# Linear attention's own-tile products as four products of 64 stationary columns a tile

## The chip, the cores and the metric

The kernel runs on one core of one Trainium2 chip. The metric is the device time of one execution, in microseconds (us). Five engines matter here: PE (TensorE: matrix products into PSUM, with its weight loads shown apart as PEld), DVE (VectorE), ACT (ScalarE), POOL (GpSimd) and SP, which issues the DMAs. A product on PE takes a stationary operand, loaded into the array (its columns become the rows, that is the partitions, of the result), and a moving operand, whose columns are streamed past it. A product whose stationary operand has 64 columns occupies one half of the array's columns and writes 64 of the 128 partitions of PSUM.

## What is computed

The reference is a layer of a diffusion backbone: 512 latent tokens and 256 context tokens of width 1024 go through one input projection, then through two branches (latent attention, and bidirectional gated linear attention with 4 heads of key and value width 128), a merge, and a gated MLP with a convolution. The change lies in the linear attention. One direction of it, for one head, cut to what matters:

```python
b_cum = jnp.cumsum(to_chunks(g), axis=3)          # log decay inside a chunk
decay, u = chunk_state_terms(kc, vc, b_cum)
s_final, s_in = scan_states(decay, u, s0)
qe = qc * jnp.exp(b_cum)
mask = jnp.tril(jnp.ones((GLA_CHUNK, GLA_CHUNK), jnp.float32))
a = jnp.einsum('bhncd,bhnsd->bhncs', qe, kc * jnp.exp(-b_cum)) * mask
o = jnp.einsum('bhncs,bhnsv->bhncv', a, vc) + jnp.einsum('bhncd,bhndv->bhncv', qe, s_in)
```

Both directions are added: a token attends forward to the tokens before it and backward to those after it, and to itself twice. The part that a chunk takes from itself (`a`) is what is called the own-tile products below; the rest comes through the state `s_in`.

## The kernel before

The kernel computes the layer in stages, each bound together by the planner of the language: `TC_KW = {"schedule_with_timeline_sim": True}` (L1562) has the order of the instructions on each engine planned from modelled costs, except where an engine's name stands in `pinned` (program order is kept) or in `behind` (instructions are put behind a named one). In the linear attention's stage nothing is pinned any more; PE's instructions only stand behind one early product (L1265). Large projections use operands split in a high and a low part; the products of the linear attention itself are plain fp32, and each of those shows as two MATMULs (two passes) with a weight load each.

The loop over the four heads (L1270 on) calls, for each head: `states`, which makes the states of both directions at the borders of the four 128-token tiles (PE products into PSUM tile `p`, ACT copies, then six DVE steps into tile `S`); `output`, which the change touches; `decay` of the next head (two scans on DVE and exponentials on ACT); projections and gates (`merge_mla`, `proj_kq`, `gate`); `gate_out`; `apply` and `to_tokens` of the next head.

`output` works on tiles of 128 tokens, as two halves c0 and c1 of 64. `K[:, 0]` and `K[:, 1]` are the keys of the forward and the backward direction (in the trace `T`), `Qp[:, 0]` and `Qp[:, 1]` the queries (in the trace `s`), all with the 128 key channels on the partitions. For each tile it makes a 128x128 block, keys on the rows and queries on the columns. The block of c0 keys and c1 queries is forward alone, that of c1 keys and c0 queries backward alone; in the two diagonal blocks both directions are needed, so there the backward product goes into `xp` and the forward one into `yp`. DVE then multiplies `xp` by `twice_diag` into `Am` (in the trace `w`), and two masked copies (COPY_PREDICATED) put the forward values of `yp` in place where the key comes before the query. Last, for each tile, the output `op` is the sum of two products of the queries `Qi` with the states (`pb<-S,s`) and one of `Am` with the values (`pb<-s,w`).

In lines L1198 to L1204 each tile has five products: one with all 128 stationary columns (`K[:, 1, cs]`) and 64 moving columns, and four with 64 stationary and 64 moving columns. In the trace these are `p<-s,T 128*128 128x64` and `p<-s,T 128*64 128x64`; the number before the star is the contraction, the number behind it the stationary columns, and the last number the moving columns.

Of the kernel before, what the change touches and what calls it, by code (L numbers as in the profile page):

```python
# [13 lines left out]
ALU = mybir.AluOpType  # L14
# [56 lines left out]
def block_kernel(ctx: ExitStack, tc: tile.TileContext, p, out):  # L71
# [3 lines left out]
    class Engine:  # L75
# [5 lines left out]
        def __getattr__(self, op):  # L81
            fn = getattr(self.eng, op)

            def call(*args, **kw):
                if self.name in behind:
                    with tc.issue_after(behind[self.name].ins):
# [6 lines left out]
    V, A, G, PE, SY = (Engine("V", nc.vector), Engine("A", nc.scalar), Engine("G", nc.gpsimd),  # L93
                       Engine("PE", nc.tensor), Engine("SY", nc.sync))
    cnt = [0]

    def tl(pool, shape, dt, tag, bufs=None):
        cnt[0] += 1
        kw = {} if bufs is None else {"bufs": bufs}
        return pool.tile(shape, dt, name=f"{tag}_{cnt[0]}", tag=tag, **kw)  # L100
# [8 lines left out]
    def pb():  # L109
        return tl(psp, [128, 512], F32, "pb", 4)  # L110

    def p2():
        return tl(psp, [128, 1024], F32, "p2", 2)
# [7 lines left out]
    def sm(n, tag, bufs=2):  # L121
        return tl(small, [128, n], F32, tag, bufs)
# [10 lines left out]
    def tt(eng, out_, a, b, op):  # L133
        return eng.tensor_tensor(out=out_, in0=a, in1=b, op=op)
# [14 lines left out]
    def mm(o, a, b, first=True, last=True):  # L149
        PE.matmul(o, lhsT=a, rhs=b, start=first, stop=last)  # L150
# [4 lines left out]
    def grp(ap, a):  # L155
        return ap.rearrange("p (a b) -> p a b", a=a)

    def rep(ap, a):

        return ap.rearrange("p (a b) -> p a b", a=1).broadcast_to([ap.shape[0], a, ap.shape[1]])  # L160

    def each(ap, n):

        return ap.rearrange("p (a b) -> p a b", b=1).broadcast_to([ap.shape[0], ap.shape[1], n])
# [19 lines left out]
    def rstd_exp(ss, n, inv_n, v=None):  # L184

        r, t = sm(n, f"rr{n}"), sm(n, f"rt{n}")
        if v is None:
            v = sm(n, f"rv{n}")
            V.tensor_scalar(out=v, in0=ss, scalar1=-0.5 * inv_n, scalar2=-0.5 * EPS, op0=ALU.mult, op1=ALU.add)
        A.activation(r, v, AF.Ln, scale=-2.0)  # L190
        A.activation(r, r, AF.Exp, scale=-0.5)
        if n == 1:
            V.tensor_scalar(out=t, in0=r, scalar1=r, scalar2=v, op0=ALU.mult, op1=ALU.mult)
            V.tensor_scalar(out=r, in0=t, scalar1=1.5, scalar2=r, op0=ALU.add, op1=ALU.mult)
        else:
            tt(V, t, r, r, ALU.mult)
            tt(V, t, t, v, ALU.mult)
            V.scalar_tensor_tensor(out=r, in0=t, scalar=1.5, in1=r, op0=ALU.add, op1=ALU.mult)
        return r
# [26 lines left out]
    twice_diag = cst[:, 130:258]  # L226
# [108 lines left out]
    with tc.tile_pool(name="e1", bufs=1) as e1:  # L335
# [309 lines left out]
        for j in range(1, 8):  # L645
            n = j + 1
# [419 lines left out]
    with tc.tile_pool(name="egl", bufs=1) as eg:  # L1066
# [9 lines left out]
        def w2():  # L1076
            return tl(eg, [128, 512], F32, "w2", 2)
# [73 lines left out]
        def vh(h, t):  # L1151
            return glav[t // 2][:, t % 2, h * 128:(h + 1) * 128]
# [35 lines left out]
        def output(h, dec, Q, St):  # L1188

            K = dec[1]
            Qp, Qi = Q
            xy = p2()
            xp, yp = xy[:, 0:512], xy[:, 512:768]
            for t in range(4):
                c0, c1 = slice(t * 128, t * 128 + 64), slice(t * 128 + 64, t * 128 + 128)
                cs = slice(t * 128, t * 128 + 128)  # L1198
                mm(xp[:, c0], K[:, 1, cs], Qp[:, 1, c0])
                mm(xp[0:64, c1], K[:, 0, c0], Qp[:, 0, c1])  # L1200
                mm(xp[64:128, c1], K[:, 1, c1], Qp[:, 1, c1])
                ys = slice(t * 64, t * 64 + 64)
                mm(yp[0:64, ys], K[:, 0, c0], Qp[:, 0, c0])
                mm(yp[64:128, ys], K[:, 0, c1], Qp[:, 0, c1])  # L1204
            Am = w2()
            tt(V, grp(Am, 4), grp(xp, 4), rep(twice_diag, 4), ALU.mult)
            for hf in range(2):
                rw = slice(64 * hf, 64 * hf + 64)
                V.copy_predicated(grp(Am, 4)[rw, :, rw], below.bitcast(I32).rearrange("p (a b) -> p a b", a=1)[rw]
                                  .broadcast_to([64, 4, 64]), grp(yp[rw, :], 4))  # L1210
            op = pb()
            for t in range(4):
                cs = slice(t * 128, (t + 1) * 128)
                mm(op[:, cs], Qi[:, 0, cs], St[:, 0, t, :], True, False)
                mm(op[:, cs], Qi[:, 1, cs], St[:, 1, t, :], False, False)
                mm(op[:, cs], Am[:, cs], vh(h, t), False, True)
            on = w2()
            A.activation(on, op, AF.Square)
            so = sm(4, "so")
            V.tensor_reduce(out=so, in_=grp(on, 4), op=ALU.add, axis=AX.X)  # L1220
            ro = rstd_exp(so, 4, 1.0 / 128)
            tt(V, grp(on, 4), grp(op, 4), each(ro, 128), ALU.mult)
            return on
# [46 lines left out]
        for h in range(GH):  # L1270
            St = states(h, dec)
            on = output(h, dec, Q, St)
            if h + 1 < GH:
                dec = decay(h + 1)
                merge_mla(2 * h)
                mod_end()
                kq = proj_kq(h + 1)
            else:
                merge_mla(2 * h)
                mod_end()  # L1280
                mod_begin(S4f)
                merge_mla(2 * h + 1)
            gate_out(h, on, gr)
            if h + 1 < GH:
                Q = apply(kq, dec)
                gr = gate(h + 1)
                to_tokens(dec)
                mod_begin(S4f)
                merge_mla(2 * h + 1)
# [138 lines left out]
    with tc.tile_pool(name="eff", bufs=1) as ef:  # L1428
# [82 lines left out]
        for t in range(4):  # L1511
# [8 lines left out]
            for i, (a, b) in enumerate(parts):  # L1520
# [11 lines left out]
                else:  # L1532

                    cs = slice(t * 128, (t + 1) * 128)
# [49 lines left out]
```

## Time and profile before

| | |
|---|---|
| median of three runs | 907.14 us (907.0 to 908.59) |
| the profiled execution's own time | 906.93 us |
| its span, from the first to the last instruction | 905.1 us |
| PE busy | 889.3 us, 98% of the span |
| DVE, ACT, POOL busy | 577.2, 395.8, 370.5 us |
| granted clock of PE | 0.998 of full speed |

The times of rows are those of the one profiled execution, in microseconds from the start of its span. The own time is the span and 1.8 us around it. A busy share is an average; what a change in one stage is worth is read from the waits and the order of time in that stage.

### The profile page before, as it was taken

What the parts mean: (1) busy time and instruction counts of PE and PEld (TensorE: products, weight loads), DVE (VectorE), ACT (ScalarE), POOL (GpSimd) and SP (SyncE); (2) the same over time, 40 slices, a digit from 0 to 9 for tenths busy, and PEclk for the clock granted to TensorE, in tenths of its full rate; (3) what the DMA queues carried; (4) which work ended last, traced back from release to release, by engine and by line L of the source; (5) the groups of instructions that cost most, each with busy time, mean ns of one, the idle gap of its engine ahead of it and who ended that gap; (6) DMA issues with size and microseconds to landing.
All of it is one profiled execution on the core that took longest, in us unless ns stands there. A gap on an engine that the chain in (4) does not pass through costs nothing.

```text
span 905.1 us, 12711 instructions
## 1 busy us (share of the span) xinstructions
PE 889.3 (98%) x4902; PEld 753.4 (83%) x4902; DVE 577.2 (64%) x970; ACT 395.8 (44%) x655; POOL 370.5 (41%) x223
## 2 busy tenths in 40 slices
PE   8999999999999999999999999999999999999996
PEld 6888899888888888888887899888888888888885
DVE  4477788775878686846774684987777776300006
ACT  4355676764353545434544333443333333322105
POOL 2512364640625252524653424343444444466403
PEclk9999999999999999999999999999999999999999
DMA  9950001224314242325972413434343432244002
GB/s 325 307 145 1 1 7 31 71 84 150 105 35 128 59 128 59 117 59 184 316 246 80 117 47 108 126 93 140 93 140 94 140 116 94 79 155 150 34 1 93
DMA packets 131436, 100.89 MB, mean 111 GB/s; under 512 B 6826, under 2 KB 121874, under 8 KB 131376
## 3 DMA queue, kind: packets, MB, share of 16 engines
q1 hardware_dynamic: 130256, 97.56, 34.9%
q0 software_dynamic: 864, 2.22, 0.7%
q8 instruction: 38, 0.62, 0.3%
q10 hardware_dynamic: 256, 0.30, 0.1%
q14 instruction: 22, 0.18, 0.1%
HBM read 97.78 MB, written 2.10 MB: 110 GB/s over the span
## 4 chain that ended last, share of the span: by engine, by line
PE 92%; DVE 3%; ACT 2%; issue 1%; POOL 1%; DMA 1%; SPq 0%; ACTq 0%; DVEq 0%; POOLq 0%
PE pb L88 49%; PE p L88 23%; PE pb L87 14%; PE p L87 6%; DMA raw<-in_w_ada_dram 1%; DVE s L88 1%; ACT P L88 0%; DVE kT L88 0%; DVE mx L88 0%; ACT s L88 0%; DVE P L88 0%; POOL P L88 0%; POOL s L88 0%; POOL wlo L88 0%; ACT kT L88 0%
## 5 line engine op out<-in xcount | busy, mean ns | idle before, releaser
L88 POOL TENSOR_TENSOR wlo<-raw,whi 128x1024 fp32r<-128x1024 f32 (+1 forms) x106 | 241.3, 2283 | 350.8 <-ACT whi L88 339.1
L88 PE MATMUL pb<-s,whi 128*128 128x512 f32 (+1 forms) x906 | 272.1, 383 | 0.0
L88 PEld LDWEIGHTS pb<-s,whi 128*128 128x128 f32 x906 | 167.3, 188 | 32.2
L88 ACT CAST whi<-raw 128x1024 fp32r<-128x1024 f32 (+1 forms) x106 | 103.2, 975 | 177.9 <-issue 78.2
L88 PE MATMUL pb<-s,wlo 128*128 128x512 f32 (+1 forms) x453 | 172.8, 381 | 0.0
L88 DVE SCALAR_TENSOR_TENSOR ac<-pb,cwT,ac 128x441 f32<-128x441 f32 (+2 forms) x160 | 110.9, 693 | 19.3 <-ACT ac L88 15.5
L87 PE MATMUL pb<-s,whi 128*128 128x512 f32 x320 | 101.8, 396 | 0.0
L88 PEld LDWEIGHTS pb<-s,wlo 128*128 128x128 f32 x453 | 85.2, 188 | 16.6
L88 PE MATMUL p<-s,s 128*128 128x512 f32 (+1 forms) x392 | 82.8, 367 | 0.6 <-DVE s L88 0.5
L88 PEld LDWEIGHTS p<-s,s 128*128 128x128 f32 x392 | 65.8, 189 | 14.0 <-issue 2.1
L87 PEld LDWEIGHTS pb<-s,whi 128*128 128x128 f32 x320 | 58.9, 188 | 12.4 <-issue 0.7
L88 PE MATMUL p<-whi,s 128*128 128x512 f32 x208 | 69.0, 393 | 0.1
L88 DVE TENSOR_TENSOR p<-p,gt 128x512 f32<-128x512 f32 x4 | 2.8, 699 | 98.5 <-PE p L88 98.4
L87 PE MATMUL pb<-s,wlo 128*128 128x512 f32 x160 | 62.8, 392 | 0.0
L88 PE MATMUL pb<-whi,s 128*128 128x512 f32 x176 | 57.6, 390 | 0.0
L88 PEld LDWEIGHTS p<-whi,s 128*128 128x128 f32 x208 | 39.0, 188 | 8.5 <-ACT s L88 0.4
L88 DVE TENSOR_TENSOR pl<-pb,ph 128x512 fp32r<-128x512 f32 x48 | 33.0, 687 | 14.8 <-ACT ph L88 14.5
L88 PE MATMUL p<-kT,s 128*128 128x512 f32 (+1 forms) x192 | 41.1, 350 | 0.9 <-ACT P L88 0.9
L88 PE MATMUL pb<-s,s 128*32 128x128 f32 (+2 forms) x322 | 41.1, 315 | 0.3 <-DMA s<-in_w_ada_dram 0.3
L88 PE MATMUL p<-wlo,s 128*128 128x512 f32 x104 | 40.5, 389 | 0.0
L88 ACT ACTIVATE ac<-ac 128x512 f32<-128x512 f32 x22 | 13.9, 632 | 60.5 <-DVE ac L88 60.5
L88 PEld LDWEIGHTS pb<-whi,s 128*128 128x128 f32 x176 | 33.1, 188 | 6.9
(248 smaller groups left out, 1564.3 us busy)
## 6 DMA issues: line engine op xcount, KB each, us to landing
raw<-in_w_up_dram SPq DMA_DIRECT2D x44, 512.0 KB, 3.7
raw<-in_w_in_dram SPq DMA_DIRECT2D x28, 512.0 KB, 3.7
raw<-in_w_down_dram SPq DMA_DIRECT2D x22, 512.0 KB, 3.6
s<-in_w_ada_dram SPq DMA_DIRECT2D x20, 512.0 KB, 5.8
raw<-in_w_ada_dram SPq DMA_DIRECT2D x18, 512.0 KB, 5.1
xn<-in_w_ada_dram SPq DMA_DIRECT2D x10, 512.0 KB, 4.8
kT<-in_w_in_dram SPq DMA_DIRECT2D x8, 320.0 KB, 6.8
s<-in_x_dram SPq DMA_DIRECT2D x4, 512.0 KB, 4.9
```

The lines of the kernel that those rows point to most:

```text
L87: return fn(*args, **kw)
L88: ins = fn(*args, **kw)
```

## The change

The five products of a tile become four, all with 64 stationary columns, written alternately to the upper and the lower half of the partitions. The product with 128 stationary columns is cut in its two halves; its upper half (c1 keys, c0 queries) is joined with the backward product of the c1 diagonal block to one product of 128 moving columns, and the forward products of c0 keys with c0 and with c1 queries are joined likewise. The results of a tile stand in 256 columns of PSUM instead of 192, so the two kinds of result are no longer in two tiles `xp` and `yp`, and the DVE multiplication and the two masked copies read them with other strides. Their number, their shapes and the values are the same.

```diff
             K = dec[1]
             Qp, Qi = Q
-            xy = p2()
-            xp, yp = xy[:, 0:512], xy[:, 512:768]
+
+            xy = grp(p2(), 4)
+            lo_, hi_ = slice(0, 64), slice(64, 128)
             for t in range(4):
+                xt = xy[:, t, :]
                 c0, c1 = slice(t * 128, t * 128 + 64), slice(t * 128 + 64, t * 128 + 128)
                 cs = slice(t * 128, t * 128 + 128)
-                mm(xp[:, c0], K[:, 1, cs], Qp[:, 1, c0])
-                mm(xp[0:64, c1], K[:, 0, c0], Qp[:, 0, c1])
-                mm(xp[64:128, c1], K[:, 1, c1], Qp[:, 1, c1])
-                ys = slice(t * 64, t * 64 + 64)
-                mm(yp[0:64, ys], K[:, 0, c0], Qp[:, 0, c0])
-                mm(yp[64:128, ys], K[:, 0, c1], Qp[:, 0, c1])
+                mm(grp(xt[hi_, :], 2)[:, :, lo_], K[:, 1, c1], Qp[:, 1, cs])
+                mm(xt[lo_, 64:192], K[:, 0, c0], Qp[:, 0, cs])
+                mm(xt[hi_, 64:128], K[:, 0, c1], Qp[:, 0, c1])
+                mm(xt[lo_, 0:64], K[:, 1, c0], Qp[:, 1, c0])
             Am = w2()
-            tt(V, grp(Am, 4), grp(xp, 4), rep(twice_diag, 4), ALU.mult)
+            tt(V, Am.rearrange("p (t b n) -> p t b n", t=4, b=2),
+               xy.rearrange("p t (b u n) -> p t b u n", b=2, u=2)[:, :, :, 0, :],
+               twice_diag.rearrange("p (t b n) -> p t b n", t=1, b=2).broadcast_to([128, 4, 2, 64]), ALU.mult)
             for hf in range(2):
                 rw = slice(64 * hf, 64 * hf + 64)
                 V.copy_predicated(grp(Am, 4)[rw, :, rw], below.bitcast(I32).rearrange("p (a b) -> p a b", a=1)[rw]
-                                  .broadcast_to([64, 4, 64]), grp(yp[rw, :], 4))
+                                  .broadcast_to([64, 4, 64]), xy[rw, :, 64:128])
```

## Rows read from the trace of the kernel before

**Rows 1.** The page: busy time of each engine, and PE's granted clock in slices.

```profile
PE 889.3 (98%) x4902; PEld 753.4 (83%) x4902; DVE 577.2 (64%) x970; ACT 395.8 (44%) x655; POOL 370.5 (41%) x223
PEclk9999999999999999999999999999999999999999
```

**Rows 2.** Waits of PE, whole kernel: who waited for whom, us, times, longest.

```profile
PE p L88 <- DVE s L88: 2.2, 3, 1.8
...
PE p L87 <- ACT T L88: 1.0, 1, 1.0
```

**Rows 3.** The chain that ended last, in order of time: start, us, what.

```profile
300.03 5.02 PE p L87 x60
305.06 4.83 PE pb L87 x22
```

**Rows 4.** Busy time of each engine from one head's products to the next's.

```profile
255.29:302.10 46.81, 46.81 (x276) 39.62 (x275) 34.74 (x53) 23.20 (x38) 17.12 (x8) 1.00 0.28 80
302.10:348.92 46.82, 46.82 (x276) 39.63 (x275) 34.72 (x53) 23.20 (x38) 18.46 (x9) 1.00 0.32 90
348.92:395.76 46.84, 46.84 (x276) 39.63 (x275) 34.80 (x54) 22.78 (x38) 18.65 (x9) 1.00 0.29 86
```

**Rows 5.** PE groups by shape, whole kernel: count, busy us, mean ns, idle before.

```profile
L87 PE MATMUL p<-s,T 128*64 128x64 f32 x128 | 7.2, 234 | 0.0
...
L87 PE MATMUL p<-s,T 128*128 128x64 f32 x32 | 6.6, 286 | 0.0
```

**Rows 6.** PE timeline, head 0, narrow looks: start, first start to last end, count.

```profile
255.18 0.33 PE L87 MATMUL p<-s,T 128*128 128x128 f32 x2
255.35 0.28 PE L87 MATMUL p<-s,T 128*128 128x64 f32 x1
255.56 0.28 PE L87 MATMUL p<-s,T 128*64 128x64 f32 x2
255.66 0.34 PE L87 MATMUL p<-s,T 128*64 128x64 f32 x6
255.94 0.32 PE L87 MATMUL p<-s,T 128*128 128x64 f32 x1
256.10 0.48 PE L87 MATMUL p<-s,T 128*128 128x64 f32 x3
256.30 0.28 PE L87 MATMUL p<-s,T 128*64 128x64 f32 x2
257.80 0.45 PE L87 MATMUL p<-s,T 128*64 128x64 f32 x8
258.18 0.49 PE L87 MATMUL pb<-S,s 128*128 128x128 f32 x2
```

**Rows 7.** PE timeline just before them: passes of 128 moving columns, 128 stationary.

```profile
253.62 0.72 PE L87 MATMUL p<-s,T 128*128 128x128 f32 x5
```

**Rows 8.** PE timeline in an early stage: 32 stationary and 128 moving columns.

```profile
15.51 0.32 PE L88 MATMUL pb<-s,s 128*32 128x128 f32 x4
15.51 0.65 PE L88 MATMUL pb<-s,s 128*32 128x128 f32 x16
```

**Rows 9.** DVE timeline around head 0's products: start, us, idle before.

```profile
255.96 1.64 DVE L88 SCALAR_TENSOR_TENSOR S<-S,ml,p 128x128 f32<-128x128 f32 x6 [1.07 <-ACT S L88]
258.30 0.69 DVE L88 TENSOR_TENSOR w<-p,cst 128x512 f32<-128x512 f32 x1 [0.70 <-PE p L87]
259.02 0.90 DVE L88 COPY_PREDICATED w<-cst,p 64x256 f32<-64x256 int32 x2
```

**Rows 10.** PE timeline, head 0: the first product that reads `Am`.

```profile
264.44 0.38 PE L87 MATMUL pb<-s,w 128*128 128x128 f32 x2
```

## The prediction

> **What bounds the kernel now.** I read the page first, then PE's waits, the chain in order of time, and at last the stretch itself. The page has PE busy for 889.3 of 905.1 us at full granted clock, with no slice below it; no other engine comes near [rows 1]. That alone would not say that PE sets the time in the linear attention, so the second view is that of PE's waits: over the whole kernel the longest sum is 2.2 us, and the one wait of line 87, where this stage's PE instructions stand, is 1.0 us, once [rows 2]. The chain that ended last runs through PE in this stage with no other engine between, the 60 MATMULs that hold the states' and the own-tile products among its pieces [rows 3]. And from the start of one head's products to the next's PE is busy for 46.81 of 46.81, 46.82 of 46.82 and 46.84 of 46.84 us, while DVE has 34.7 to 34.8, ACT about 23 and POOL 17 to 19 [rows 4]. So a microsecond taken from PE here is a microsecond of the span, as long as nobody else becomes late.
>
> How much PE time the products have is in the groups by shape: 128 passes of 64 stationary columns, 7.2 us, and 32 of 128 columns, 6.6 us [rows 5]; 13.8 us in four heads. Although they are a quarter as many, the whole ones take nearly as much. The last view shows why.
>
> **What a tile costs now.** The narrow looks give starts [rows 6]. The pass of the whole product at 255.35 is followed by a pair of half ones at 255.56: 0.21 us, where a pass of 64 columns has 0.06 in a run of such passes (below). So 0.15 us goes into the change from 128 to 64 stationary columns. The two passes of the pair start within 0.01 us of each other: they are on the two halves of the array and run at once. The next passes start at 255.66, 0.10 later; six of them end 0.34 later, and one lasts 0.22 (its group's mean is 0.234 [rows 5]), so three pairs start within 0.12 us: 0.06 a pair. The first pair costs 0.10 because its weight load has nothing to hide behind; after that the loads are hidden. From the last pair, at 255.66 + 0.12 = 255.78, to the next whole product at 255.94 is 0.16, of which about 0.10 is the change back. Its two passes lie 0.16 apart (255.94 and 256.10), again with a first load in the open, and the next pair is at 256.30. A tile lasts from 255.56 to 256.30, or by three tiles (255.56 to 257.80) 0.747 us: 0.10 + 0.06 + 0.06 + 0.16 for the halves and 0.16 + 0.21 for the whole product. All of it, from the last pass of the states at 255.18 to the first product with the states at 258.18, is 3.00 us.
>
> **What a tile costs after.** Each half of the array gets one product of 128 and one of 64 moving columns, that is two passes of each. A pass of 64 columns is 0.06 as above. A pass of 128 moving columns on one half is not in the trace. With 128 stationary columns five of them take 0.72 us, and with 0.275 for the last, (0.72 - 0.275)/4 = 0.111 a pass [rows 7]. With 32 stationary columns sixteen passes on four quarters take 0.65, where the first four take 0.32: three further rounds in 0.33, or 0.11 a round, with four streams at once [rows 8]. Both neighbours say 0.11 and I take it; the second shows that several streams of 128 columns run beside one another. As bounds I keep 0.107 and 0.122 (all sixteen spread over the rounds, (0.65 - 0.28)/3, with start-up in it), that is 8 passes a half by -0.004 or +0.011, or -0.03 to +0.09 us a head. A tile then costs 2 x 0.11 + 2 x 0.06 = 0.34 us.
>
> One head, from the last pass of the states on: that pass and the change to 64 columns 0.11 + 0.15 = 0.26; the first pass with its load in the open 0.16 (as between 255.94 and 256.10); the rest of tile 0 0.11 + 0.06 + 0.06 = 0.23; tiles 1 and 2 0.68; tile 3 up to the start of its last pass 0.11 + 0.11 + 0.06 = 0.28; the second half's lag 0.01; the change back 0.15 (257.80 + 0.45 - 0.22 = 258.03, to 258.18). Sum 1.77 us. It was 3.00, so 1.23 us a head go, and **4.9 us** in four heads. Of that, three pairs of changes of the array's width are most: 3 x (0.15 + 0.10) = 0.75; joining narrow products and the freed whole ones make up the rest.
>
> **What moves with it.** The DVE multiplication (0.69 us) and the two masked copies (0.90) read other strides [rows 9]. The trace has no such read of PSUM; I take no change, with bounds from nothing to twice their time, 1.6 us a head. Either way it is covered: `Am` is ready at 259.92, and the first product that reads it starts at 264.44 [rows 10], so 4.5 us lie between, filled with products of other parts. If that cover were gone, each 0.1 us would count on PE. No wait and no DMA is added; the last product of the group releases DVE as before. What is late next: DVE's six state steps end at 257.60 and DVE idles 0.70 us for the products [rows 9]. They will end near 256.95, so the multiplication starts right behind the state steps, 0.70 us earlier, while PE is 1.23 earlier. Against PE the DVE chain loses 0.53 us of its 4.5, and 2.1 with the 1.6 of the upper bound. ACT and POOL have over 20 us free in each head [rows 4]. After the stage PE goes on without waits of more than 2.2 us in total for any one releaser [rows 2], so I see nobody who would hold the gain back.
>
> By the rows, then, 906.93 - 4.92 = 902.0 for the profiled execution; the median of the three runs stands 0.21 above that one, so the forecast is 902.2 us.
>
> **The rivals.** *Loads in the open.* If a weight load were hidden only behind a product on other rows of the array, each pass on the halves, all of which use all 128 rows, would pay what the first pair pays: 0.10 instead of 0.06, more exactly 0.05 as the first pass of a group shows against the others. Fifteen further passes a half would cost 0.75 a head, 3.0 in all: 905.2 us. The pairs at 0.06 in [rows 6] speak against it. The Trainium skill states this rule (TensorE: Matmul & The Clock Gate, section "The mechanism" of Part 3: loads overlap products in flight only when the row group differs). By it the sum would be 905.2, by the rows 902.2; the trace does not agree with it, at 0.06 us a pair with 64 columns.
>
> *Passes in strict order.* If a product's second pass had to start before the other half's first, the halves would overlap in part only: 0.40 a tile instead of 0.34, 0.9 us in all, 903.1. Two starts within 0.01 us at 255.56, and four on four quarters [rows 8], speak against it.
>
> *The change doesn't do what it says.* The halves take turns with 128 moving columns: 0.68 a tile, 0.26 + 0.05 + 4 x 0.68 - 0.06 + 0.15 = 3.12 a head, 0.5 slower in all, 907.6, no change. [Rows 8] speak against it.
>
> *The planner takes the cover away (slower).* The order on PE is planned from modelled costs. If, with shorter products, it puts the products that read `Am` right behind them, PE waits for DVE: the state steps end at 257.60, multiplication and copies add 0.03 + 0.69 + 0.03 + 0.90 + 0.05, so `Am` is there at 259.30. PE is through at 256.95 and has one product with the states (0.45) that can go first: 1.9 us of waiting a head, 7.6 in four, 902.2 + 7.6 = 909.8. It decides for slower when less than about 0.2 us of other work a head is left between; now there are 6.3 (258.18 to 264.44). In two of the four heads it would be 3.8: 906.0, no change. The wide cover speaks against both.
>
> **How the numbers follow.** Forecast 902.2: 0.80. Loads in the open 905.2: 0.03. Strict order 903.1: 0.03. Halves in turn 907.6: 0.03. Planner in all heads 909.8: 0.05; in part of them 906.0: 0.06. About 0.2% (1.8 us, some 905.3 to 909.0) is what a measurement of this kernel can tell from no change. Faster: 0.80 + 0.03 and part of the loads' case, 0.84; same 0.10; slower 0.06. The range: downward 0.4 us for the drains or first loads if cheaper (0.15 and 0.05 a head, half of them), 0.1 for the pass, and about a microsecond for the planner's small shifts and the spread of the runs (907.0 to 908.59): 900.7. Upward it takes in strict order and loads in the open, 905.3. What is left out is the halves in turn and the planner's cases, 0.14.
>
> **What the profile after would show.** Groups `p<-s,T 128*64 128x128` and `128*64 128x64` with 64 passes each and no `128*128 128x64`; starts in pairs, 0.34 us a tile, and 1.77 us from the last pass of the states to the first product with them. The heads' period falls from 46.8 to 45.6 us with PE still busy throughout. DVE's idle time before the multiplication is gone. Wrong would be shown by: a tile at 0.40 or 0.68 (order, turns), passes of 64 columns 0.10 apart (loads), a PE wait for DVE's `w` at line 87 (planner), or the period at 45.6 and a new wait later on.

## The result, and the profile after

The changed kernel takes 901.85 us (median of four runs, 901.79 to 901.94) against 907.12 us (907.0 to 908.59) for the kernel before: a ratio of 0.9937, with a 95% interval of 0.9926 to 0.9948. The profiled execution took 901.90 us, of which its span is 900.1; before it was 906.93 and 905.1. Some executions of every other kernel here, of the one before too, lie 1.4 to 2.5 us above its lowest, mostly at a slightly lower granted clock (0.993 to 0.997, where the others have 0.995 to 0.998), so for the experiments the lowest run of each stands beside the lowest run of the kernel before in the same series.

The groups of PE by shape, whole kernel (count, busy us, mean ns, idle before), which answer to [rows 5]:

```profile
L87 PE MATMUL p<-s,T 128*64 128x128 f32 x64 | 5.8, 280 | 0.0
L87 PE MATMUL p<-s,T 128*64 128x64 f32 x64 | 4.5, 220 | 0.0
```

The passes with 128 stationary and 64 moving columns are gone. What was 7.2 and 6.6 us of PE is 5.8 and 4.5, 3.5 us less by this view, and PE's busy time on the page falls from 889.3 to 883.6. A group's busy time depends on how overlapping passes are put down to one shape or another, so I go by the starts. The narrow looks at the PE timeline in head 0 (start, first start to last end, count) answer to [rows 6]:

```profile
255.28 0.28 PE L87 MATMUL p<-s,T 128*128 128x128 f32 x1
...
255.49 0.33 PE L87 MATMUL p<-s,T 128*64 128x128 f32 x2
...
255.65 0.50 PE L87 MATMUL p<-s,T 128*64 128x128 f32 x7
...
255.87 0.45 PE L87 MATMUL p<-s,T 128*64 128x128 f32 x6
...
256.54 0.39 PE L87 MATMUL p<-s,T 128*64 128x128 f32 x4
...
256.98 0.38 PE L87 MATMUL pb<-S,s 128*128 128x128 f32 x1
```

The last pass of the states starts at 255.28, the first pair of half products at 255.49, its second pass at 255.65. Tile 1 begins at 255.87 and tile 3 at 256.54: two tiles in 0.67, or 0.335 us a tile where it was 0.747. The first product with the states starts at 256.98, 1.69 us after the last pass of the states; before it was 3.00. In all four heads the trace gives 1.69 (1.693 or 1.694), so 1.30 us a head and 5.2 us in all. The first period from one head's first product with the states to the next's, with the columns of [rows 4]:

```profile
256.98:302.51 45.53, 45.53 (x271) 38.68 (x267) 33.37 (x54) 23.00 (x38) 18.38 (x8) 1.00 0.31 87
```

PE is still busy for all of it, and the period is 45.53 instead of 46.81 to 46.84; the next two are 45.53 and 45.54, with PE busy throughout. PE's waits, with the columns of [rows 2], have nothing new in the stage; line 87 has the one that it had:

```profile
PE p L87 <- ACT T L88: 1.0, 1, 1.0
```

The DVE timeline around the products, as [rows 9], and the first product that reads `Am`, as [rows 10]:

```profile
257.62 0.69 DVE L88 TENSOR_TENSOR w<-p,cst 128x512 f32<-128x512 f32 x1
258.38 0.48 DVE L88 TENSOR_SCALAR C<-pb,pcol 128x256 f32<-128x256 f32 x1
258.78 0.90 DVE L88 COPY_PREDICATED w<-cst,p 64x256 f32<-64x256 int32 x2
```

```profile
263.94 0.39 PE L87 MATMUL pb<-s,w 128*128 128x128 f32 x2
```

The multiplication follows the state steps with no idle time, and the steps with other strides take the same 0.69 and 0.90 us. The planner now puts a step of the decay between them, so `Am` is ready at 259.68; PE reads it at 263.94, 4.3 us later.

### The profile page after: what moved, and what is told of

It is laid out like the page before. It is cut to its first block, busy times and chain, and to the rows that moved or that the text cites. A ratio compares the mean times of both kernels' runs of the same rounds, so it can differ in the third digit from the quotient of the medians.

```text
span 900.1 us, 12647 instructions
## 1 busy us (share of the span) xinstructions
PE 883.6 (98%) x4870; PEld 749.1 (83%) x4870; DVE 569.1 (63%) x970; ACT 396.2 (44%) x655; POOL 369.1 (41%) x223
## 4 chain that ended last, share of the span: by engine, by line
PE 92%; DVE 3%; ACT 2%; issue 1%; POOL 1%; ACTq 0%; DVEq 0%; POOLq 0%
PE pb L88 49%; PE p L88 23%; PE pb L87 14%; PE p L87 6%; DVE s L88 1%; ACT P L88 1%; ACT ph L88 0%; DVE kT L88 0%; DVE mx L88 0%; ACT s L88 0%; DVE P L88 0%; POOL P L88 0%; POOL s L88 0%; POOL wlo L88 0%; ACT kT L88 0%
```

## The experiments

The theory: the gain is PE time in this group alone, most of it from changing the array between 128 and 64 stationary columns once a head instead of four times, and it reaches the end because PE is busy throughout and DVE's part is covered. The rivals: the gain comes from having fewer products; the order written has to alternate strictly; DVE's part or the planner's order decides. The table sets what the traces give (from the last pass of the states to the first product with them, times four heads) beside the measured gain.

| kernel | states to first product, us | gain by rows, 4 heads | lowest run | lowest of before, same series | gain |
|---|---|---|---|---|---|
| before | 3.00 | | | | |
| changed | 1.69 | 5.2 | 901.79 | 907.0 | 5.2 |
| wholes first | 2.13 | 3.5 | 903.43 | 906.72 | 3.3 |
| cut only | 1.75 | 5.0 | 901.85 | 906.72 | 4.9 |
| same half | 1.74 | 5.0 | 901.85 | 906.72 | 4.9 |
| narrow first | 1.70 | 5.2 | 901.52 | 906.72 | 5.2 |
| two tiles | 2.18 | 3.3 | 903.68 | 906.86 | 3.2 |
| four tiles | 2.75 | 1.0 | 905.85 | 906.86 | 1.0 |

In seven kernels the gain by the lowest runs is what the rows of this one stretch give, within 0.2 us. By the medians the gains are 5.3, 3.4, 3.3, 4.2, 5.1, 4.2 and 2.9 in the order of the table, up to 1.9 away from the rows, so the times alone would not carry this. The traces do without that choice: a head's period, between the last passes of the states of heads 0 and 3 divided by three, is 46.82 us before and falls by 1.29, 0.87, 1.26, 1.26, 1.31, 0.79 and 0.28, where the stretch alone falls by 1.30, 0.87, 1.24, 1.25, 1.30, 0.81 and 0.25. That is the strongest support for reading a change here as PE time, one for one.

**Wholes first.** The kernel before, with only the order of its products changed.

```diff
-                mm(xp[:, c0], K[:, 1, cs], Qp[:, 1, c0])
+                if t == 0:
+                    for u in range(4):
+                        mm(xp[:, u * 128:u * 128 + 64], K[:, 1, u * 128:u * 128 + 128], Qp[:, 1, u * 128:u * 128 + 64])
                 mm(xp[0:64, c1], K[:, 0, c0], Qp[:, 0, c1])
```

> The kernel before with its own twenty products a head, only in another order: the four products with 128 stationary columns first, then the sixteen with 64. That leaves one change of the array's width in and one out for a head instead of four of each. Theory (the width changes, with the first load behind each, are most of what the change saved): from the last pass of the states to the first product with them 1.80 to 2.14 us instead of 3.00 (0.11 + seven whole passes at 0.058 to 0.107 + 0.205 + 0.107 + fourteen rounds at 0.058 + 0.16), so 0.86 to 1.20 a head less, 902.3 to 903.7 us. Rival (the saving comes from having fewer products, four a tile instead of five): the same twenty products, so no saving, 907 us and about 3.0 us a head.

Median 903.55 us, ratio 0.9962 (0.9947 to 0.9977); 2.13 us a head. The same twenty products in another order give two thirds of the gain (0.87 of 1.30 us a head), so the rival falls. The PE timeline of head 0, narrow looks:

```profile
255.31 0.45 PE L87 MATMUL p<-s,T 128*128 128x64 f32 x3
...
255.37 0.50 PE L87 MATMUL p<-s,T 128*128 128x64 f32 x3
...
256.04 0.28 PE L87 MATMUL p<-s,T 128*128 128x64 f32 x1
...
256.24 0.28 PE L87 MATMUL p<-s,T 128*64 128x64 f32 x2
```

The three whole passes from 255.37 on take 0.50 us, one of them lasts 0.275: they start (0.50 - 0.275)/2 = 0.11 apart, though each streams only 64 columns, as far apart as passes of 128 [rows 7]. The streaming is not what takes this time: the first of the eight, at 255.31, is followed after 0.06 (0.058 by the trace). The weight loads of these passes are 0.11 apart, in the view of PEld:

```profile
255.31 0.75 PEld L87 LDWEIGHTS p<-s,T 128*128 128x128 f32 x6
```

Six loads, of which the last takes 0.19, start (0.75 - 0.19)/5 = 0.11 apart, so the passes seem to go at the rate of their loads of 128 columns; no run here changes the loads alone. The last whole pass starts at 256.04 and the first pair at 256.24, 0.205 by the trace. With 0.11 for the pass that is 0.09 for the change of width, with 0.06 for its streaming it is 0.15; what the rows show is the 0.205, behind a last pass of 64 moving columns here and of 128 in the changed kernel (255.28 to 255.49) alike.

**Cut only.** The kernel before, with the whole product cut in two and nothing joined.

```diff
-                mm(xp[:, c0], K[:, 1, cs], Qp[:, 1, c0])
+                mm(xp[0:64, c0], K[:, 1, c0], Qp[:, 1, c0])
+                mm(xp[64:128, c0], K[:, 1, c1], Qp[:, 1, c0])
```

> The kernel before with only the product of 128 stationary columns cut in two of 64, nothing joined: six products a tile, all of 64 moving columns, alternately on the lower and the upper half. Theory (width changes): 0.205 + 0.107 + 22 rounds at 0.058 + 0.16 = 1.75 us from the last pass of the states to the first product with them, 0.06 more than the changed kernel's 1.69, so 902.1 us. Rival (fewer products save): six a tile are more than five, so no less than the 907 us of before.

1.75 us a head, as expected to the hundredth, and 0.37 less than with the wholes first; lowest run and profiled execution 901.85, median 903.62, ratio 0.9954 (0.994 to 0.9967). Six products a tile do nearly as well as four. Joining, and with it the new layout in PSUM and the new strides of the DVE steps, is worth 0.06 us a head, 0.24 in all, by the rows; the times can't tell that apart.

**Same half.** The changed kernel with the second and third product of a tile exchanged.

```diff
                 mm(grp(xt[hi_, :], 2)[:, :, lo_], K[:, 1, c1], Qp[:, 1, cs])
-                mm(xt[lo_, 64:192], K[:, 0, c0], Qp[:, 0, cs])
                 mm(xt[hi_, 64:128], K[:, 0, c1], Qp[:, 0, c1])
+                mm(xt[lo_, 64:192], K[:, 0, c0], Qp[:, 0, cs])
                 mm(xt[lo_, 0:64], K[:, 1, c0], Qp[:, 1, c0])
```

> The changed kernel with the four products of a tile in another order: both of the upper half, then both of the lower, instead of alternately. Theory (PE looks past a product whose half is busy, each half has its own line): the same 0.335 us a tile and 901.9 us. Rival (products start in order, so the order written has to alternate): only one round of a tile overlaps with the next half, 2 x 0.32 - 0.055 = 0.585 us a tile, 1.0 us more a head, 905.9 us.

1.74 us a head, lowest run 901.85, median 902.71, ratio 0.9948 (0.9934 to 0.9962). The PE timeline of head 0, at the start of the group:

```profile
255.40 0.45 PE L87 MATMUL p<-s,T 128*64 128x128 f32 x4
```

The four passes of 128 moving columns of a tile, two of each half, start within 0.45 - 0.27 = 0.18 us, before any of the upper half's second product. The theory holds: PE starts the lower half's product past the upper half's second one. The tile stays at 0.335; the lower half ends half a round, 0.05, later. How far it looks is the question of the next two.

**Two tiles, four tiles.** The upper half's products of two tiles, or of all four, written together, then the lower half's. The diff shows four tiles; with two, the same pair of loops stands twice, over (0, 1) and (2, 3).

```diff
-            for t in range(4):
+            for t in (0, 1, 2, 3):
...
                 mm(grp(xt[hi_, :], 2)[:, :, lo_], K[:, 1, c1], Qp[:, 1, cs])
+                mm(xt[hi_, 64:128], K[:, 0, c1], Qp[:, 0, c1])
+            for t in (0, 1, 2, 3):
...
                 mm(xt[lo_, 64:192], K[:, 0, c0], Qp[:, 0, cs])
-                mm(xt[hi_, 64:128], K[:, 0, c1], Qp[:, 0, c1])
                 mm(xt[lo_, 0:64], K[:, 1, c0], Qp[:, 1, c0])
```

> The changed kernel with the products of the upper half of two tiles written together (four), then the four of the lower half. In the run with two and two, PE started the other half's first product 0.013 us behind, past one product that waited for its half, and fell back by half a round later. Theory (PE looks past waiting products of one half as far as some window reaches, and a few products are within it): the same 0.335 us a tile, the lower half behind the upper by at most a tile: 1.75 to 2.0 us from the last pass of the states to the first product with them, 902 to 903 us. Rival (it looks past one product only): two tiles overlap in part, 0.335 x 4 + 2 x 0.5 = 2.3 to 2.7 us a head, 904.5 to 906 us.

> The changed kernel with all eight products of the upper half of a head written first, then all eight of the lower. Theory (a window of more than eight products): still both halves at once, 1.75 to 2.1 us a head, 902 to 903.5 us. Rival (products in order, or a window of a few): the halves one after the other but for the window, up to 0.205 + 2 x 1.33 + 0.16 = 3.0 us a head, as long as before the change, 907 us.

2.18 and 2.75 us a head; lowest runs 903.68 and 905.85, ratios 0.9954 (0.9932 to 0.9977) and 0.9975 (0.9964 to 0.9987). With four tiles the halves run one after the other but for one tile at the seam; that the upper half runs alone for 1.06 us first shows that the planner kept the order written. The PE timeline of that kernel before the seam and at it:

```profile
257.92 0.44 PE L87 MATMUL p<-s,T 128*64 128x128 f32 x3
...
258.26 0.49 PE L87 MATMUL p<-s,T 128*64 128x128 f32 x6
```

Before it three passes start within 0.44 - 0.22 = 0.22 us, one stream; from 258.26 six start within 0.49 - 0.22 = 0.27, two streams. The lower half's first pass (258.264 by the trace) starts 0.006 us after the upper half's last tile begins, with three passes of that tile still waiting; it did not start a pass earlier, with four waiting. With two tiles and in the same-half kernel the other half also starts with three passes waiting. So PE here looks past three waiting passes and not past four, one less than a half has in a tile. For two tiles neither side of the expectation came: 2.18 lies between the 2.0 of the theory and the 2.3 of the rival. For four the theory falls and the rival, a window of a few, holds. Written alternately, as in the change, that much is never needed: each start passes one waiting pass of the other half.

**Narrow first.** The changed kernel with the products of 64 moving columns ahead of those of 128 in each tile.

```diff
+                mm(xt[hi_, 64:128], K[:, 0, c1], Qp[:, 0, c1])
+                mm(xt[lo_, 0:64], K[:, 1, c0], Qp[:, 1, c0])
                 mm(grp(xt[hi_, :], 2)[:, :, lo_], K[:, 1, c1], Qp[:, 1, cs])
                 mm(xt[lo_, 64:192], K[:, 0, c0], Qp[:, 0, cs])
-                mm(xt[hi_, 64:128], K[:, 0, c1], Qp[:, 0, c1])
-                mm(xt[lo_, 0:64], K[:, 1, c0], Qp[:, 1, c0])
```

> The changed kernel with the two products of 64 moving columns of each tile ahead of the two of 128. The group then ends with passes of 128 columns instead of 64. Theory (a change of the array's width takes a fixed time from the start of the last pass, as the 0.205 on entry showed after passes of 64 and of 128 columns alike): 0.152 on the way out as before, so the group is shorter by one streamed pass, 0.05 us a head, 1.64 us, 901.65 us. Rival (on the way out the time counts from the end of the last pass): 0.20 on the way out, 1.69 us a head, 901.85 us.

1.70 us a head, median 901.88, ratio 0.9943 (0.9931 to 0.9955). The end of the group:

```profile
256.67 0.27 PE L87 MATMUL p<-s,T 128*64 128x128 f32 x1
256.87 0.38 PE L87 MATMUL pb<-S,s 128*128 128x128 f32 x1
```

0.20 us lie between the last pass and the first product with the states, where 0.15 lie behind a pass of 64 columns. My theory falls, the rival holds: on the way out the change takes about 0.09 on top of the last pass (0.11 or 0.06). On the way in the same 0.09 comes out where the last pass is counted at 0.11.

**No cover.** The changed kernel, with PE's later work put behind the products that read `Am`.

```diff
-                mm(op[:, cs], Am[:, cs], vh(h, t), False, True)
+                last = PE.matmul(op[:, cs], lhsT=Am[:, cs], rhs=vh(h, t), start=False, stop=True)
+            behind["PE"] = last
```

> The changed kernel with every later PE instruction of the linear attention put behind the last product that reads Am, so that the products of other parts which lay between them can no longer do so. Theory (that work is the cover of DVE's steps; without it PE waits): PE is free of the own-tile products at 256.98 in head 0 and Am is ready near 259.3 to 259.7, with one product with the states (0.45) ahead of it: 1.9 to 2.3 us of waiting a head for DVE's w, 7.6 to 9.1 in all, 909.5 to 911 us. Rival (the cover isn't needed, PE finds other work or the time is made up later): 901.9 us.

Median 907.82 us, 1.0011 of before (1.0002 to 1.002): 6 us above the changed kernel, all of the gain gone. PE's waits in that kernel:

```profile
PE pb L87 <- DVE w L88: 4.1, 4, 1.0
...
PE pb L87 <- DVE S L88: 1.2, 4, 0.3
```

and the PE timeline of head 0:

```profile
256.88 0.49 PE L87 MATMUL pb<-S,s 128*128 128x128 f32 x2
257.66 0.49 PE L87 MATMUL pb<-S,s 128*128 128x128 f32 x2 [0.29 <-DVE S L88]
259.18 0.49 PE L87 MATMUL pb<-s,w 128*128 128x128 f32 x2 [1.03 <-DVE w L88]
```

The mechanism is as expected: the two waits add up to 5.3 of the 6 us. The price is 1.32 us of waiting a head and not 1.9 to 2.3: the first product with `Am` starts 2.30 us after the group, as worked out (2.35), but two products with the states come ahead of it, not one.

**DVE five times.** The changed kernel with the multiplication written five times.

```diff
-            tt(V, Am.rearrange("p (t b n) -> p t b n", t=4, b=2),
...
+            for _ in range(5):
+                tt(V, Am.rearrange("p (t b n) -> p t b n", t=4, b=2),
...
```

> The changed kernel with DVE's multiplication into Am written five times over instead of once, 4 x 0.69 = 2.8 us more DVE work a head between the own-tile products and the masked copies. Theory (DVE has 4 us of cover against PE there): no wait at Am; at most the decay steps behind it become late at the next head's transposes, where 1.8 us are left, 1.0 us in each of three heads: 901.9 to 904.9 us. Rival (DVE's steps count, as they would if the other strides made them slower): 2.8 a head, 11 us, 912.9 us.

Median 901.61 us (lowest 901.40, against 906.75 for before), ratio 0.9939 (0.9923 to 0.9956): no cost. DVE's copies and the product that reads `Am`, in head 0:

```profile
264.06 0.90 DVE L88 COPY_PREDICATED w<-cst,p 64x256 f32<-64x256 int32 x2
```

```profile
267.45 0.36 PE L87 MATMUL pb<-s,w 128*128 128x128 f32 x1
```

`Am` is ready at 264.97, 5.3 us later than in the changed kernel, and PE reads it at 267.45 instead of 263.94: the planner moved the reader by 3.5 us, and 2.5 us lie between the two where 4.3 did. So the reader's place is not fixed, it moves with the planned cost of DVE's steps. The price of slower DVE steps at an unmoved order was not shown by this.

## Why the prediction was right

It said 902.2 us, and 901.85 came.

*PE bounds the stage, one for one.* Right. The periods fell with PE busy throughout, and over seven kernels the gain follows the rows of the stretch from 1.0 to 5.2 us.

*The width changes are most of it.* Right in kind, and mis-sized in one term. Behind the whole product of the kernel before, the way in was 0.205 us from the start of its last pass; the prediction took 0.06 of it for the pass, put 0.15 down to the change, and added this to the 0.11 of a last pass of 128 moving columns. But 0.205 came behind that pass too: the way in, counted from the start of the last pass, does not grow with that pass's moving columns. In the sum after the change that put 0.26 where 0.205 came; it is the one term that was off by more than a hundredth, and it makes 1.77 against 1.69 with the tile's 0.34 against 0.335, 0.3 us in four heads. Of these 0.3 the profiled execution shows 0.1 (901.90 against the 902.0 of the sum); the spread of the runs is larger than either, so that the total came this near is in part luck. The stated 0.75 a head for three changes of width agrees with neither part alone: with whole passes counted at 0.11 a change is 0.09 each way, and three pairs are 0.55. Reordering saved 0.87, because after each change a first load also lies in the open (0.05 each way, 0.3 for three pairs). What the prediction called the rest is 0.37 for cutting the whole products and 0.06 for joining.

*The pass of 128 moving columns on a half takes 0.11, both halves at once.* Right: 0.11 (half of what a tile of 0.335 has beside two passes of 0.056), as the rows with 128 and with 32 stationary columns both gave. Halves in turn did not occur; the four-tiles kernel shows that they do, for all but one tile, where the order written does not alternate.

*The first pass 0.16, the way out 0.15.* Right: 0.160 and 0.152.

*DVE's steps cost nothing.* Right; the same durations, and the multiplication began at 257.62, behind the state steps without idle time, where 257.60 was worked out.

*The rivals.* Loads in the open: the narrow passes stay at 0.056 a round with only the first load showing, so they did not come. That loads overlap a product in flight only in other row groups, as TensorE: Matmul & The Clock Gate of the Trainium skill has it ("The mechanism"), is not what these traces show for two halves of the columns. Strict order: did not come, and would not have been strict either; the look past three passes was not in my view of it. The planner's rival was built on a real wait, but priced too high: the no-cover kernel lost 6.0 us, to 907.8, no change against before and not the 909.8 that I gave as slower. The planner did move a little: the reader of `Am` in head 0 starts 6.96 us after the first product with the states instead of 6.26, with three more passes of a projection ahead of it, to no effect that the rows show.

## What to carry to other kernels

Where products with 128 and with 64 stationary columns alternate on PE, look at the starts across each change before counting products or columns: here each change cost about 0.09 us and a first weight load in the open (0.05), and sorting the products by width alone, with the arithmetic untouched, gave two thirds of the gain. A run of products with few moving columns on the whole array can go at the rate of its weight loads: 0.11 us a pass of 64 moving columns here, where two halves at once took 0.06. Write products of different halves alternately, or at most two in a row on one half, and check that the work planned behind the group is still there: without it the whole gain went into waits for DVE.

## What the runs showed of the hardware that I had not expected

PE's start of products on the other half reaches past three waiting passes, not four; that decides between 1.74 and 2.75 us for the same eight and eight products. In a run, passes with 128 stationary and 64 moving columns start 0.11 us apart, as those with 128 moving columns do, and so do their weight loads; only the first of the run was followed after 0.06. And a step of another engine can get shorter with no effect: of the two scans of the decay the DVE timeline has, before and after (start, first start to last end of both),

```profile
269.71 6.59 DVE L88 TENSOR_TENSOR_SCAN T<-s,T 128x512 f32<-128x512 f32 x2
```

```profile
270.41 4.50 DVE L88 TENSOR_TENSOR_SCAN T<-s,T 128x512 f32<-128x512 f32 x2
```

2.1 us less in this head and in each of the next two, and the page has 8.1 us less of DVE in all (577.2 to 569.1). One scan of the two is shorter, 1.2 us instead of 3.3. In the ten traces here every scan of the decay beside which 2.2 us or more of POOL's work run takes 3.3, and every one with 1.1 or less takes 1.2; in the no-cover kernel, with next to none, both take 1.2. That POOL's work is the cause was not tried by itself. As PE bounds the stage, the time shows nothing of it.
